# One step of a hybrid diffusion backbone: key latents inside the last block, adaLN rows turned later, a convolution's tanh in a slot of its own

## The chip, the cores and the metric

The kernel runs on one core of one Trainium2 chip. The metric is the time of the device for one execution, in microseconds (us). The core has a matrix engine (TensorE, PE in the profile), a vector engine (VectorE, DVE), a scalar engine (ScalarE, ACT), a third elementwise engine (GpSimd, POOL) and a queue engine that here issues the transfers (SyncE, SP). Each runs its own list of instructions in order; semaphores join them. PE writes its results into banks of PSUM, and a bank can be written again only when another engine has read it.

## What is computed

Two layers over 1024 latent tokens (with a grid position) and 256 context tokens, 1280 in all, width 1024. Each layer is RMSNorm, an adaLN shift and scale, a mixer, and a gated residual. The first mixer has windowed attention (A) and a matrix memory (mLSTM, B) side by side, the second is latent attention (C). What the change touches:

```
def _adaln(cond, w, b):
    m = jax.nn.silu(cond) @ w + b
    shift, scale, gate = jnp.split(m[:, None, :], 3, axis=-1)
...
    qk = jax.nn.silu(_dwconv_centred(jnp.concatenate([q, k], axis=-1), conv_w))   # mixer B
...
    q = (_rmsnorm(qa, q_norm) @ w_qb).reshape(B, T, C_HEADS, C_NOPE + C_ROPE)     # mixer C
    c_kv = _rmsnorm(kva, kv_norm)
    keys_ckv = jnp.concatenate([c_kv, cc], axis=1)
    keys_kr = jnp.concatenate([_axial_rope(kr, rows, cols), ckr[:, :, None, :]], axis=1)
    kv = (keys_ckv @ w_kvb).reshape(B, Tk, C_HEADS, C_NOPE + C_VDIM)
```

In C the keys are 1536: 1280 of the step (latents of width 256) and 256 from a cache.

## The kernel before

**Numbers.** Every float32 operand of a product is split into a high part in a shorter float type (fp32r) and the low rest, and a product is three matmuls: high x high, high x low, low x high. So each operand that is made costs a cast on ACT (names with h) and a subtraction on DVE or POOL (names with l): L576/L577 for weights, L1648/L1649 for v of mixer B, L820/L821 for the rotary parts of C, L2070/L2071 and L2067/L2068 for latents, keys, queries and values of C.

**Order.** The program is written as one stream. In three stretches (the start, the memory of B with dense blocks beside it, the windowed attention) the stream is the order, written by hand (`manual_schedule`). In the rest, to which the first layer's dense blocks behind the start and the entry of mixer C belong, the build itself sets in what order each engine gets the instructions, and only the dependencies are given.

**Dense blocks.** Products with the input weights go in blocks of 256 to 384 columns. A unit is one PSUM bank: 24 matmuls, eight depths of 128 by three. Tokens come in three chunks, 512, 512 and 256 (`CHUNKS`), or in ten tiles of 128 (tt). Beside the blocks run steps of the adaLN sums (`mod_sums`, L501 to L551): 64 small matmuls make four rows of sums in a bank, `columns` (L512) scales them on ACT (mrow, L514), turns them on PE (the transpose of L123) and adds the bias on DVE (B or A, L521). In the same stretch `gates` makes the memory's gates: scans over 1280 tokens on DVE (L1528 to L1535), then exponentials on ACT (gB, rst, gM; L1563, L1567, L1570), then turns of LI, rst and gM on PE, ten of them into each bank, copied out at L1591.

**Convolution of B** (`b_proj`, L1595). For each head the q and k blocks are followed by a convolution over three tokens. It goes in slots: `K.later(f, n)` puts f into the slot n further on; a slot holds the work of some unit and of the memory beside it. `taken` copies a bank into a ring tile (scr, L1609); a slot or more later `conv` (L1622) takes one of four cx tiles and writes the middle tap on ACT (L1626); a slot later `taps` adds the two others on DVE (L1629, L1630) and at once issues the tanh on ACT (L1632); a slot later `silu` multiplies on DVE (L1636); a slot later a transfer writes cx out (in<-cx, L154 on SP). Behind q and k come the units of v, which `v_split` casts on ACT (L1648) and subtracts on DVE (L1649).

**Entry of C** (`layer_c`). The last two dense blocks make the query latents (b = 0) and the key latents (b = 1), tile by tile (`latent`, L1987). A dict `K.behind` gives functions to run behind a tile (b, tt): `q_latent` turns the query latents of a chunk, `q_rope` (L2032) makes the rotary query part for four heads and one chunk (nine matmuls, then the rotation L770 to L773 and the split L820/L821), and `k_rope` the same for the keys' rotary part (32 rows). After the last unit the rest follows: `kv_latent` (L2020) turns the key latents of chunk 0, 1, 2 and of the cache (3) into the ckv tiles, four `q_rope`s for chunk 2, one `k_rope`, the weights' splits (L2278 to L2297), then `C.keys`, `C.queries` and `C.values`. The normalised tokens of the layer (hh0, hl0 and so on, chunk by chunk) are last read by the dense blocks.

Of the kernel before, what the change touches and what calls it, by code (L numbers as in the profile page):

```python
# [12 lines left out]
F32R = mybir.dt.float32r  # L13
# [13 lines left out]
KD = D // 128  # L27
# [473 lines left out]
def mod_sums(K, p, blocks):  # L501


    nc, cond = K.nc, cond_cols(K, p)
    at = lambda t, c: t[c::32]
    if any(f < 2 * D for _, f in blocks):
        bcol = K.t(p, [128, 16], F32, "bcol1", 1)
        K.dma(bcol, K.I["k_cols"][:, 96:112])
        nc.vector.tensor_scalar(bcol[:, 8:16], bcol[:, 8:16], 1.0, None, ALU.add)
        K.A[1], K.Bm[1] = [K.const.tile([128, 2, 8], F32, tag=f"{n}1", name=f"{n}1") for n in "AB"]  # L510

    def columns(ps, f):  # L512
        rows = K.t(p, [128, 128], F32, "mrow1", 2)
        nc.scalar.mul(rows, ps[:, 0:128], 0.5)  # L514
# [6 lines left out]
        nc.vector.tensor_add(dst, src, bc(bcol, 8 * a))  # L521
        if a:
            nc.vector.tensor_mul(dst, dst, bc(K.gcol, 8))

    def gate(ps, l, f, bias):
        nc.vector.scalar_tensor_tensor(bias, ps[:, 0:128], 0.5, bias, ALU.mult, ALU.add)
        for c in range(2):
            K.dma(K.modd[l][c, f:f + 512].rearrange("(q p) -> q p", p=128), at(bias, c))

    for l, f in blocks:  # L530
        ws, bias = [], None
        for i in range(8):
            for k in (2 * i, 2 * i + 1) if i < 4 else ():
                w = K.t(p, [128, 512], F32, "mw", 8)
                K.dma(w, K.I["w_mod"][l, k * 128:(k + 1) * 128, f:f + 512])
                ws.append(w)
            if i == 4 and f >= 2 * D:
                bias = K.t(p, [128, 128], F32, "bmod", 2)
                nc.gpsimd.memset(bias, 0.0)
                for c in range(2):  # L540
                    K.dma(at(bias, c), K.I["b_mod"][l, f:f + 512].rearrange("(q p) -> q p", p=128))
            if i == 7:
                ps = K.ps()
                for k in range(KD):
                    for q in range(4):
                        K.mm(ps[q * 32:q * 32 + 32, 0:128], cond[:, k, :], ws[k][:, q * 128:(q + 1) * 128], k == 0, k == KD - 1)
                if bias is None:
                    columns(ps, f)
                else:
                    gate(ps, l, f, bias)  # L550
            yield  # L551


class DenseBlock:
# [295 lines left out]
def layer_ab(K):  # L850
    nc, I = K.nc, K.I
    left, right = K.left, K.right
    d = K.d = {}
# [12 lines left out]
    hp = right("hT0")  # L866
# [93 lines left out]
        pass  # L960
    while opened:
        opened.pop().release()
    hp = K.hp1 = right("hT1")
    K.hTh, K.hTl = [], []
    for ci, (t0, N) in enumerate(CHUNKS):
        K.hTh.append(hp.tile([128, KD, N], F32R, tag=f"hh{ci}", name=f"h1Th{ci}"))
        K.hTl.append(hp.tile([128, KD, N], F32R, tag=f"hl{ci}", name=f"h1Tl{ci}"))
    wp = K.w1 = right("w1")
# [626 lines left out]
def b_proj(K, wp, h):  # L1595
# [26 lines left out]
    def conv(p, ci, qk, j):  # L1622
        t0, N = CHUNKS[ci]
        cw = K.cw[:, :, qk * 8 + 2 * h + j]
        x = K.t(K.cvp, [128, 512], F32, "cx", 4)[:, 0:N]
        nc.scalar.mul(x, p[:, 1:N + 1], cw[:, 1:2])  # L1626

        def taps():
            nc.vector.scalar_tensor_tensor(x, p[:, 0:N], cw[:, 0:1], x, ALU.mult, ALU.add)  # L1629
            nc.vector.scalar_tensor_tensor(x, p[:, 2:N + 2], cw[:, 2:3], x, ALU.mult, ALU.add)  # L1630
            th = K.sc(K.ring, [128, 512], F32, "cth")[:, 0:N]
            nc.scalar.activation(th, x, AF.Tanh, scale=1.0 if qk == 0 else 16.0)  # L1632
# [441 lines left out]
def layer_c(K):  # L2074
# [42 lines left out]
    for w, o in zip(pre, (0, 0, 256)):  # L2117
        K.dma(w, I["w_kvb_c"][0, :, o:o + 256].rearrange("(k p) (h a c) -> p k h a c", p=128, h=2, a=2))
    K.u = {}
    K.behind = {(0, 5): [partial(q_latent, K, 0)], (0, 9): [partial(q_latent, K, 1)], (1, 1): [partial(q_latent, K, 2)]}  # L2120
    for n in range(8):
        K.behind[1, n + 2] = [partial(q_rope, K, wr, n % 4, n // 4)]
    K.behind[1, 5].append(partial(k_rope, K, 0))
    K.behind[1, 9].append(partial(k_rope, K, 1))
    dense.run(2)
    K.w1.release()
    K.hp1.release()

    lp = right("lat")
    ckv = [[lp.tile([128, 2, 512], F32R, tag=f"ckv{s}{c}", name=f"ckv{s}{c}") for c in range(3)] for s in range(2)]  # L2130
    wp = right("cw")
    sets = [right("ckv0"), right("cvr")]
    C = Mla(K, wp, cq, ckv)
    C.weights(0, pre[0])
    C.weights_v(0, pre[1:])
    k_rope(K, 2)
# [93 lines left out]
class Mla:  # L2230
# [298 lines left out]
```

## Time and profile before

| what | value |
|---|---|
| median of 3 runs | 2583.2 us (2578.94, 2583.2, 2584.51) |
| the profiled execution | 2579.96 us, of which the span of the instructions is 2578.2 us |
| mean granted PE clock | 0.996 |
| HBM read and written | 233.49 MB and 110.50 MB |

PE is the busiest engine by far; how much of the span each engine is busy stands in the prediction's first lines. The page's busy rows by slices (40 slices of 64 us) show where the others come near it: DVE and ACT in the last third, which is the attention of C. A row of the waits' view reads: engine, operation and line that waited, then what it waited for, then us in total, times, and the longest. A row of a timeline reads: start, length, engine, line, operation, out<-in, how many, and in brackets the idle time before it and what ended that. A row of a stretch reads: from and to, length, busy us of each engine (and instructions), granted clock of PE (1.00 is full), share of the DMA engines, GB/s.

### The profile page before, as it was taken

What the parts mean: (1) busy time and instruction counts of PE and PEld (TensorE: products, weight loads), DVE (VectorE), ACT (ScalarE), POOL (GpSimd) and SP (SyncE); (2) the same over time, 40 slices, a digit from 0 to 9 for tenths busy, and PEclk for the clock granted to TensorE, in tenths of its full rate; (3) what the DMA queues carried; (4) which work ended last, traced back from release to release, by engine and by line L of the source; (5) the groups of instructions that cost most, each with busy time, mean ns of one, the idle gap of its engine ahead of it and who ended that gap; (6) DMA issues with size and microseconds to landing.
All of it is one profiled execution on the core that took longest, in us unless ns stands there. A gap on an engine that the chain in (4) does not pass through costs nothing.

```text
span 2578.2 us, 48626 instructions
## 1 busy us (share of the span) xinstructions
PE 2534.9 (98%) x16482; PEld 2248.8 (87%) x16482; DVE 1702.8 (66%) x3927; ACT 1442.0 (56%) x3664; POOL 1126.9 (44%) x1510
## 2 busy tenths in 40 slices
PE   8999999999999999999999999999999999999998
PEld 6998998998998888878888778898899999999887
DVE  6633655656657575677777456426888888888754
ACT  6423535535434432577666433233888888888842
POOL 6223233233225344366554543135455555555832
PEclk9999999999999999999999999999999999999999
DMA  7665576666577564465443455423210101101334
GB/s 267 209 196 162 155 215 180 182 202 178 160 220 225 182 215 150 113 171 161 127 124 97 162 160 165 126 70 120 66 39 28 43 28 43 33 30 28 122 100 133
DMA packets 338955, 347.21 MB, mean 135 GB/s; under 512 B 36409, under 2 KB 281838, under 8 KB 338450
## 3 DMA queue, kind: packets, MB, share of 16 engines
q1 hardware_dynamic: 338706, 344.10, 43.8%
q8 instruction: 131, 2.15, 0.3%
q14 instruction: 118, 0.97, 0.1%
HBM read 233.49 MB, written 110.50 MB: 133 GB/s over the span
## 4 chain that ended last, share of the span: by engine, by line
PE 89%; DVE 3%; DMA 2%; ACT 2%; issue 2%; POOL 1%; SPq 1%; POOLq 0%; DVEq 0%; ACTq 0%
PE mm L119 36%; PE S L119 31%; PE V L119 9%; PE T L123 7%; PE D L119 3%; PE mm L123 3%; PE T L119 1%; SPq L154 1%; POOL w L1068 0%; DMA w<-in_w_out_c 0%; DMA w<-in_w_out_ab 0%; DMA y<-w 0%; POOL wl L577 0%; DMA xin<-in_x_sample 0%; DVE gM L1535 0%
## 5 line engine op out<-in xcount | busy, mean ns | idle before, releaser
L577 POOL TENSOR_TENSOR wl<-wf,wh 128x256 fp32r<-128x256 f32 (+2 forms) x272 | 222.8, 845 | 496.7 <-ACT wh L576 432.9
L119 PE MATMUL mm<-hTh,wh 128*128 128x512 f32 (+1 forms) x912 | 329.2, 361 | 0.9 <-DVE scr L821 0.9
L119 PE MATMUL mm<-hTh,wl 128*128 128x512 f32 (+1 forms) x912 | 324.7, 356 | 0.0
L119 PE MATMUL mm<-hTl,wh 128*128 128x512 f32 (+1 forms) x912 | 324.1, 355 | 0.0
L119 PE MATMUL S<-cK,cQ 96*128 96x512 f32 (+3 forms) x1248 | 301.6, 365 | 0.8 <-ACT cPb L2421 0.4
L2469 DVE TENSOR_TENSOR cpl<-T,cph 128x512 fp32r<-128x512 f32 x336 | 227.8, 684 | 36.3 <-ACT cph L2468 32.5
L119 PEld LDWEIGHTS S<-cK,cQ 96*128 96x128 f32 (+1 forms) x1248 | 192.5, 189 | 20.7 <-ACT cPb L2421 1.7
L2468 ACT CAST cph<-T 128x512 fp32r<-128x512 f32 x336 | 192.4, 589 | 29.1 <-PE T L123 15.7
L119 PEld LDWEIGHTS mm<-hTh,wl 128*128 128x128 f32 x912 | 171.4, 188 | 27.0
L119 PEld LDWEIGHTS mm<-hTh,wh 128*128 128x128 f32 x912 | 171.5, 188 | 23.8 <-DVE scr L821 1.1
L119 PEld LDWEIGHTS mm<-hTl,wh 128*128 128x128 f32 x912 | 171.7, 188 | 23.2
L2419 DVE TENSOR_REDUCE cmx<-S 128x1 f32<-128x512 f32 x256 | 172.9, 682 | 20.6 <-PE S L119 18.9
L119 PE MATMUL V<-cph,cV 128*128 128x256 f32 x672 | 177.3, 289 | 1.0 <-ACT cph L2468 0.9
L119 PE MATMUL V<-cpl,cV 128*128 128x256 f32 x672 | 171.9, 284 | 0.8 <-DVE cst L2396 0.3
L1343 ACT CAST att_ph<-mm 128x512 fp32r<-128x512 f32 x168 | 98.6, 587 | 94.4 <-PE mm L123 92.6
L2400 POOL TENSOR_SCALAR cPa<-cPa,cst 128x512 f32<-128x512 f32 x128 | 98.3, 768 | 114.5 <-DVE cst L2397 94.3
L119 PE MATMUL mm<-wh,hTh 128*128 128x256 f32 x480 | 136.2, 284 | 3.3 <-DVE scr L1649 3.2
L1344 DVE TENSOR_TENSOR att_pl<-mm,att_ph 128x512 fp32r<-128x512 f32 x168 | 115.8, 689 | 35.7 <-ACT att_ph L1343 30.8
L119 PE MATMUL mm<-wl,hTh 128*128 128x256 f32 x480 | 135.7, 283 | 0.1
L119 PE MATMUL mm<-wh,hTl 128*128 128x256 f32 x480 | 135.2, 282 | 0.0
L119 PEld LDWEIGHTS V<-cph,cV 128*128 128x128 f32 x672 | 126.6, 188 | 7.9 <-ACT cph L2468 1.1
L119 PEld LDWEIGHTS V<-cpl,cV 128*128 128x128 f32 x672 | 126.7, 189 | 6.7 <-DVE cpl L2469 0.9
(459 smaller groups left out, 7737.1 us busy)
## 6 DMA issues: line engine op xcount, KB each, us to landing
wf<-in_w_in_ab SPq DMA_DIRECT2D x120, 256.0 KB
in<-in SPq DMA_DIRECT2D x40, 514.0 KB
in<-in SPq DMA_DIRECT2D x32, 386.0 KB
mw<-in_w_mod SPq DMA_DIRECT2D x48, 256.0 KB
in<-scr SPq DMA_DIRECT2D x40, 258.0 KB
o_x<-y SPq DMA_DIRECT2D x20, 512.0 KB
xin<-in_k_wmod SPq DMA_DIRECT2D x16, 512.0 KB
in<-cx SPq DMA_DIRECT2D x32, 256.0 KB
```

The source lines that it names most:

```text
L119: return self.nc.tensor.matmul(out, lhsT, rhs, start=start, stop=stop)
L123: self.nc.tensor.transpose(out, in_, self.ident[:p, :p])
L154: self.nc.sync.dma_start(f(out), f(in_))
L577: K.nc.gpsimd.tensor_sub(wl, wf[:, k], wh.bitcast(F32))
L1343: K.nc.scalar.copy(ph, self.T)
L1344: K.nc.vector.tensor_sub(pl, self.T, ph.bitcast(F32))
L2400: nc.gpsimd.tensor_scalar(pv, pv, wt[:, c:c + 1], rd, ALU.mult, ALU.mult)
L2419: nc.vector.tensor_reduce(mx[:, b, c:c + 1], S, AX.X, ALU.max, negate=True)
L2468: nc.scalar.copy(ph, T_)
L2469: nc.vector.tensor_sub(pl, T_, ph.bitcast(F32))
```

## The change

Three edits. (1) `columns` no longer turns its rows at once: it returns a function that does (`turned`), and the next block of adaLN sums calls it at its third step (i == 2); the last is called at the end. (2) In the convolution the tanh is put one slot behind the taps; the silu and the transfer behind it move a slot as well. (3) In layer C the first chunk of tokens gets a pool of its own (K.lat, tag hT1), and the tiles hh0 and hl0 are taken again for the key latents (`keys_latent`), so that `kv_latent` of chunk 0, 1 and the cache can run inside the last block, behind tiles (1, 5), (1, 9) and (1, 7). The eight `q_rope`s of chunks 0 and 1 get other places, two of them in the block before; the four of chunk 2 follow `kv_latent(2)` together. Two of the seven V tiles are the unused quarters of hh0 and hl0.

```
--- before.py
+++ after.py
@@ -512,6 +512,9 @@
     def columns(ps, f):
         rows = K.t(p, [128, 128], F32, "mrow1", 2)
         nc.scalar.mul(rows, ps[:, 0:128], 0.5)
+        return partial(turned, rows, f)
+
+    def turned(rows, f):
         pc = K.psT()
         K.tr(pc[:, 0:128], rows)
         a, k = f // D, f % D // 128
@@ -527,9 +530,12 @@
         for c in range(2):
             K.dma(K.modd[l][c, f:f + 512].rearrange("(q p) -> q p", p=128), at(bias, c))
 
+    late = None
     for l, f in blocks:
         ws, bias = [], None
         for i in range(8):
+            if i == 2 and late:
+                late = late()
             for k in (2 * i, 2 * i + 1) if i < 4 else ():
                 w = K.t(p, [128, 512], F32, "mw", 8)
                 K.dma(w, K.I["w_mod"][l, k * 128:(k + 1) * 128, f:f + 512])
@@ -545,10 +551,12 @@
                     for q in range(4):
                         K.mm(ps[q * 32:q * 32 + 32, 0:128], cond[:, k, :], ws[k][:, q * 128:(q + 1) * 128], k == 0, k == KD - 1)
                 if bias is None:
-                    columns(ps, f)
+                    late = columns(ps, f)
                 else:
                     gate(ps, l, f, bias)
             yield
+    if late:
+        late()
 
 
 class DenseBlock:
@@ -960,9 +968,11 @@
         pass
     while opened:
         opened.pop().release()
-    hp = K.hp1 = right("hT1")
+    K.lat = right("hT1")
+    hp = K.hp1 = right("hT2")
     K.hTh, K.hTl = [], []
     for ci, (t0, N) in enumerate(CHUNKS):
+        hp = K.hp1 if ci else K.lat
         K.hTh.append(hp.tile([128, KD, N], F32R, tag=f"hh{ci}", name=f"h1Th{ci}"))
         K.hTl.append(hp.tile([128, KD, N], F32R, tag=f"hl{ci}", name=f"h1Tl{ci}"))
     wp = K.w1 = right("w1")
@@ -1628,6 +1638,9 @@
         def taps():
             nc.vector.scalar_tensor_tensor(x, p[:, 0:N], cw[:, 0:1], x, ALU.mult, ALU.add)
             nc.vector.scalar_tensor_tensor(x, p[:, 2:N + 2], cw[:, 2:3], x, ALU.mult, ALU.add)
+            K.later(tanh)
+
+        def tanh():
             th = K.sc(K.ring, [128, 512], F32, "cth")[:, 0:N]
             nc.scalar.activation(th, x, AF.Tanh, scale=1.0 if qk == 0 else 16.0)
             K.later(lambda: silu(th))
@@ -2117,32 +2130,43 @@
     for w, o in zip(pre, (0, 0, 256)):
         K.dma(w, I["w_kvb_c"][0, :, o:o + 256].rearrange("(k p) (h a c) -> p k h a c", p=128, h=2, a=2))
     K.u = {}
+    ckv = [[], []]
+
+    def keys_latent(ci):
+        if not ci:
+            for t, nm in zip(ckv, ("hh0", "hl0")):
+                whole = K.t(K.lat, [128, KD, 512], F32R, nm)
+                t += [whole[:, k:k + 2, :] for k in range(0, KD, 2)]
+        kv_latent(K, ci, ckv)
+
     K.behind = {(0, 5): [partial(q_latent, K, 0)], (0, 9): [partial(q_latent, K, 1)], (1, 1): [partial(q_latent, K, 2)]}
-    for n in range(8):
-        K.behind[1, n + 2] = [partial(q_rope, K, wr, n % 4, n // 4)]
-    K.behind[1, 5].append(partial(k_rope, K, 0))
-    K.behind[1, 9].append(partial(k_rope, K, 1))
+    for n, at in enumerate(((0, 7), (0, 8), (1, 0), (1, 2), (1, 3), (1, 4), (1, 6), (1, 8))):
+        K.behind.setdefault(at, []).append(partial(q_rope, K, wr, n % 4, n // 4))
+    for f, ci, at in ((k_rope, 0, (1, 5)), (k_rope, 1, (1, 9))):
+        K.behind.setdefault(at, []).append(partial(f, K, ci))
+    for ci, tt in ((0, 5), (3, 7), (1, 9)):
+        K.behind.setdefault((1, tt), []).append(partial(keys_latent, ci))
     dense.run(2)
     K.w1.release()
     K.hp1.release()
 
-    lp = right("lat")
-    ckv = [[lp.tile([128, 2, 512], F32R, tag=f"ckv{s}{c}", name=f"ckv{s}{c}") for c in range(3)] for s in range(2)]
+    lp = K.lat
+    spare = [t.pop().rearrange("p k (i g a d) -> p (k i) g a d", i=2, g=2, a=2) for t in ckv]
     wp = right("cw")
     sets = [right("ckv0"), right("cvr")]
     C = Mla(K, wp, cq, ckv)
     C.weights(0, pre[0])
     C.weights_v(0, pre[1:])
     k_rope(K, 2)
-    for ci in range(4):
-        kv_latent(K, ci, ckv)
-        q_rope(K, wr, ci, 2)
+    kv_latent(K, 2, ckv)
+    for q in range(4):
+        q_rope(K, wr, q, 2)
     C.add_set(sets[0])
     p.release()
     cu.release()
     ap = C.ap = left("catt")
     C.add_queries(ap)
-    C.add_values(ap, sets[1])
+    C.add_values(ap, sets[1], spare=spare)
     for c in range(3):
         C.keys(0, c)
     C.queries(0, 0)
@@ -2249,11 +2273,11 @@
                 K.dma(keys[1][s][o:o + 32, :], kr[s])
         self.KV.append(keys)
 
-    def add_values(self, *pools):
+    def add_values(self, *pools, spare):
 
         n = 0
-        tiles = []
-        for pool, k in zip(pools, (3, 4)):
+        tiles = [*spare]
+        for pool, k in zip(pools, (3, 2)):
             tiles += [pool.tile([128, 4, 2, 2, 64], F32R, tag=f"cV{i}", name=f"cV{i}") for i in range(n, n + k)]
             n += k
         self.V = {(p, c): tiles[i] for p, row in enumerate(self.SLOTS) for c, i in enumerate(row)}
```

In the built program, on DVE, at the first adaLN row in the stretch with the gates: before, the bias add B stands right behind a tap of the convolution and ahead of v's constants (scr<-unit).

```order
L1630 SCALAR_TENSOR_TENSOR cx_1865<-scr_1861,cw,cx_1865 128x256
L521 TENSOR_TENSOR B_1144<-T_2017,bcol_242_1140 128x4x2
L1568 TENSOR_TENSOR dl<-dl,mp 36x10
L1650 CAST scr_1977<-unit 128x2x2
L1650 CAST scr_2032<-unit 128x2x2
```

On DVE at the same place, now:

```order
L1649 SCALAR_TENSOR_TENSOR cx_1865<-scr_1869,cx_1865 128x256
L1662 TENSOR_TENSOR scr_1977<-S_1913,scr_1977 128x256
L1662 TENSOR_TENSOR scr_2029<-S_1926,scr_2029 128x256
L1662 TENSOR_TENSOR scr_2046<-S_1939,scr_2046 128x256
L1662 TENSOR_TENSOR scr_2067<-S_1952,scr_2067 128x256
L1663 CAST scr_2142<-unit 128x2x2
L524 TENSOR_TENSOR B_1144<-T_2106,bcol_242_1140 128x4x2
L1662 TENSOR_TENSOR scr_2101<-S_2076,scr_2101 128x256
```

The add has moved behind the silu and four low parts of v (scr, from the banks S). On PE, the turn of the row itself (T<-ident,mrow; S are the banks of v's units) before:

```order
L119 MATMUL S_1939<-wh_1487,hTh_127 128x256
L123 MATMUL T_2017<-ident,mrow_366_2015 128x128
L119 MATMUL S_1939<-wl_1488,hTh_127 128x256
L119 MATMUL S_1939<-wh_1487,hTl_128 128x256
L119 MATMUL S_1952<-wh_1475,hTh_127 128x256
```

And on PE now, with the turn 38 rows later, behind the whole next unit of v:

```order
L119 MATMUL S_2076<-wl_1488,hTh_129 128x256
L119 MATMUL S_2076<-wh_1487,hTl_130 128x256
L123 MATMUL T_2106<-ident,mrow_366_2015 128x128
L119 MATMUL S_2113<-wh_1455,hTh_129 128x256
L119 MATMUL S_2113<-wl_1456,hTh_129 128x256
```

Here the two last matmuls of one unit, all twelve of the next one's second half and the 24 of a further unit have come ahead of the turn.

On ACT in the memory stage, at the last head's change from k to v, before (ho and kwh belong to the memory, mm are the banks of v):

```order
L1860 ACTIVATE ho_9317<-S_9211,hr_9313 128x256
L1626 ACTIVATE cx_9319<-scr_9153,cw 128x256
L1632 ACTIVATE scr_9323<-cx_9236 128x512
L1648 CAST scr_9327<-mm_9173 128x256
L1648 CAST scr_9331<-mm_9186 128x256
L1648 CAST scr_9335<-mm_9268 128x256
```

On ACT, now:

```order
L1873 ACTIVATE ho_9313<-S_9207,hr_9309 128x256
L1636 ACTIVATE cx_9315<-scr_9149,cw 128x256
L1645 ACTIVATE scr_9321<-cx_9147 128x512
L1661 CAST scr_9323<-mm_9169 128x256
L1661 CAST scr_9327<-mm_9182 128x256
L1661 CAST scr_9331<-mm_9264 128x256
L1803 CAST sd_9387<-um_8990 128x2x128
L1811 CAST Ch_9390<-Cs_8106 128x516
L1645 ACTIVATE scr_9396<-cx_9232 128x512
```

The tanh ahead of the three casts belongs to another buffer: cx_9147, whose taps are in the slot before. That of the newest 512 tokens (cx_9232, scr_9396) has moved behind the casts.

On PE at the entry of C, now, from the keys' products (S from hh and hl, which hold the latents) to the first queries (mm from cq):

```order
L119 MATMUL S_22696<-hh_4699_22306,wkl_22566 128x512
L119 MATMUL S_22696<-hh_4699_22306,wkh_22565 128x512
L123 MATMUL T_22584<-ident,u_22446 128x128
L119 MATMUL S_22696<-hl_4700_22307,wkh_22565 128x512
L119 MATMUL S_22696<-hh_4699_22306,wkl_22566 128x512
L123 MATMUL T_22589<-ident,u_22446 128x128
L123 MATMUL T_22584<-ident,u_22505 128x128
L123 MATMUL T_22589<-ident,u_22505 128x128
L119 MATMUL mm_23026<-cq_20447,wqh_22561 128x512
```

Before, the queries stood behind nine further rows of turns and products; the last q_ropes now stand ahead of this piece. On POOL at the same place, now (wkl, wvl and wql are the low parts of weights, rp_s and rp_t the rotation, ur a power):

```order
L2306 TENSOR_TENSOR wkl_22566<-wk_21517,wkh_22565 128x256
L2321 TENSOR_TENSOR wvl_22570<-wk_21518,wvh_22569 128x2x128
L2321 TENSOR_TENSOR wvl_22570<-wk_21519,wvh_22569 128x2x128
L780 TENSOR_TENSOR rp_s_22524<-rp_s_22524,rtabc 32x512
L2011 TENSOR_TENSOR ur_22510<-ur_22510,mhalf 128x1
L829 TENSOR_TENSOR rp_t_22469<-rp_t_22469,so_h_22475 128x512
L2303 TENSOR_TENSOR wql_22562<-wq_22559,wqh_22561 128x384
L781 TENSOR_TENSOR rp_t_22523<-rp_t_22523,rp_s_22524 32x512
L2017 TENSOR_TENSOR cko_22515<-u_22505,kvb 128x256
```

The rotation of the second k_rope's part (rp_s and rp_t of 32 rows) stands with the weights' low parts in one queue, its sum (rp_t<-rp_t,rp_s) behind wql; before, one more rotation 128 wide stood between them.

More of the change, by code (lines that the diff above doesn't have):

```diff
@@ L514, in columns, with turned @@
         nc.scalar.mul(rows, ps[:, 0:128], 0.5)
+        return partial(turned, rows, f)
+    def turned(rows, f):
         pc = K.psT()
@@ L528, in gate @@
             K.dma(K.modd[l][c, f:f + 512].rearrange("(q p) -> q p", p=128), at(bias, c))
+    late = None
     for l, f in blocks:
@@ L532, in mod_sums @@
         for i in range(8):
+            if i == 2 and late:
+                late = late()
             for k in (2 * i, 2 * i + 1) if i < 4 else ():
@@ L547, in mod_sums @@
                 if bias is None:
-                    columns(ps, f)
+                    late = columns(ps, f)
                 else:
@@ L551, in mod_sums @@
             yield
+    if late:
+        late()
 class DenseBlock:
@@ L962, in layer_ab @@
         opened.pop().release()
-    hp = K.hp1 = right("hT1")
+    K.lat = right("hT1")
+    hp = K.hp1 = right("hT2")
     K.hTh, K.hTl = [], []
     for ci, (t0, N) in enumerate(CHUNKS):
+        hp = K.hp1 if ci else K.lat
         K.hTh.append(hp.tile([128, KD, N], F32R, tag=f"hh{ci}", name=f"h1Th{ci}"))
@@ L1630, in taps, with tanh @@
             nc.vector.scalar_tensor_tensor(x, p[:, 2:N + 2], cw[:, 2:3], x, ALU.mult, ALU.add)
+            K.later(tanh)
+        def tanh():
             th = K.sc(K.ring, [128, 512], F32, "cth")[:, 0:N]
@@ L2119, in layer_c, with keys_latent @@
     K.u = {}
-    K.behind = {(0, 5): [partial(q_latent, K, 0)], (0, 9): [partial(q_latent, K, 1)], (1, 1): [partial(q_latent, K, 2)]}
[L2121 to L2124, printed above, removed]
+    ckv = [[], []]
+    def keys_latent(ci):
+        if not ci:
+            for t, nm in zip(ckv, ("hh0", "hl0")):
+                whole = K.t(K.lat, [128, KD, 512], F32R, nm)
+                t += [whole[:, k:k + 2, :] for k in range(0, KD, 2)]
+        kv_latent(K, ci, ckv)
+    K.behind = {(0, 5): [partial(q_latent, K, 0)], (0, 9): [partial(q_latent, K, 1)], (1, 1): [partial(q_latent, K, 2)]}
+    for n, at in enumerate(((0, 7), (0, 8), (1, 0), (1, 2), (1, 3), (1, 4), (1, 6), (1, 8))):
+        K.behind.setdefault(at, []).append(partial(q_rope, K, wr, n % 4, n // 4))
+    for f, ci, at in ((k_rope, 0, (1, 5)), (k_rope, 1, (1, 9))):
+        K.behind.setdefault(at, []).append(partial(f, K, ci))
+    for ci, tt in ((0, 5), (3, 7), (1, 9)):
+        K.behind.setdefault((1, tt), []).append(partial(keys_latent, ci))
     dense.run(2)
@@ L2127, in layer_c @@
     K.hp1.release()
-    lp = right("lat")
-    ckv = [[lp.tile([128, 2, 512], F32R, tag=f"ckv{s}{c}", name=f"ckv{s}{c}") for c in range(3)] for s in range(2)]
+    lp = K.lat
+    spare = [t.pop().rearrange("p k (i g a d) -> p (k i) g a d", i=2, g=2, a=2) for t in ckv]
     wp = right("cw")
@@ L2136, in layer_c @@
     k_rope(K, 2)
-    for ci in range(4):
-        kv_latent(K, ci, ckv)
-        q_rope(K, wr, ci, 2)
+    kv_latent(K, 2, ckv)
+    for q in range(4):
+        q_rope(K, wr, q, 2)
     C.add_set(sets[0])
@@ L2144, in layer_c @@
     C.add_queries(ap)
-    C.add_values(ap, sets[1])
+    C.add_values(ap, sets[1], spare=spare)
     for c in range(3):
@@ L2250, in add_set, with add_values @@
         self.KV.append(keys)
-    def add_values(self, *pools):
+    def add_values(self, *pools, spare):
         n = 0
-        tiles = []
-        for pool, k in zip(pools, (3, 4)):
+        tiles = [*spare]
+        for pool, k in zip(pools, (3, 2)):
             tiles += [pool.tile([128, 4, 2, 2, 64], F32R, tag=f"cV{i}", name=f"cV{i}") for i in range(n, n + k)]
```

## The prediction

> **What bounds the kernel now.** I read the page's busy times first, then the view of what TensorE (PE) waited for, then the busy time and granted clock in chosen stretches of 3.41 us, and only then the timelines around each wait.
>
> ```profile
> span 2578.2 us, 48626 instructions
> PE 2534.9 (98%) x16482; PEld 2248.8 (87%) x16482; DVE 1702.8 (66%) x3927; ACT 1442.0 (56%) x3664; POOL 1126.9 (44%) x1510
> PE T L123 <- ACT mrow L514: 5.0, 2, 4.6
> PE mm L119 <- DVE scr L1649: 3.2, 1, 3.2
> PE T L123 <- DVE ckv L2071: 1.8, 4, 0.6
> ```
>
> PE is busy for 2534.9 of 2578.2 us. No matmul is removed by the change, so it can win only from the 43.3 us of idle and from time that PE ran on a halved clock. The change aims at three places: the adaLN rows (5.0 us in 2 waits, the longer 4.6), one eviction in the convolution stage (3.2 us), and the entry of the last layer (ckv and its neighbours). The second cost is in the stretches (columns: length, then busy us of PE, PEld, DVE, ACT, POOL, then granted clock, DMA share, GB/s):
>
> ```profile
> 138.44:141.86 3.42, 0.00 (x1) 0.00 (x0) 3.29 (x7) 1.51 (x4) 0.36 (x1) 1.00 0.81 176
> 145.27:148.69 3.42, 3.42 (x18) 3.42 (x18) 2.94 (x10) 2.63 (x3) 0.00 (x0) 0.50 0.84 185
> 148.69:152.10 3.41, 3.41 (x30) 3.41 (x30) 2.33 (x8) 1.75 (x7) 0.00 (x0) 1.00 0.96 318
> 677.75:681.16 3.41, 0.44 (x3) 0.44 (x4) 3.02 (x8) 2.66 (x8) 0.20 (x1) 1.00 0.22 71
> 681.16:684.58 3.42, 3.42 (x18) 3.42 (x17) 2.81 (x7) 0.84 (x2) 0.00 (x0) 0.50 0.62 216
> 1148.80:1155.60 6.80, 5.40 (x34) 3.99 (x33) 5.26 (x14) 5.45 (x14) 3.34 (x5) 1.00 0.74 216
> 1790.50:1793.91 3.41, 1.51 (x9) 0.79 (x8) 2.57 (x6) 2.79 (x7) 2.68 (x3) 1.00 0.35 126
> 1793.91:1800.74 6.83, 6.19 (x16) 4.63 (x16) 3.11 (x9) 2.65 (x8) 3.40 (x7) 0.50 0.63 177
> 1786.00:1800.74 14.74, 11.28 (x44) 7.82 (x43) 8.81 (x19) 7.76 (x17) 9.94 (x12) 0.77 0.50 153
> 1700.00:1786.00 86.00, 86.00 (x558) 82.45 (x557) 39.94 (x87) 31.71 (x85) 37.74 (x44) 1.00 0.21 66
> ```
>
> A stretch with 3.42, 2.97 (3.41 - 0.44) or 1.90 (3.41 - 1.51) us of PE idle is followed by one at clock 0.50; the two from 1148.80 with 1.40 together (6.80 - 5.40) are at 1.00 and stay there. So a stall costs itself and, from somewhere between 1.4 and 1.9 us in one stretch, a half-clock stretch too. Its price: PE gets through 18 matmuls instead of 30 in 3.4 us, a loss of 0.4 x 3.41 = **1.4 us** for each such stretch of work.
>
> **The adaLN rows (first edit).**
>
> ```profile
> 143.04 0.48 PE L123 MATMUL T<-ident,mrow 128*128 128x128 f32 x1 [4.59 <-ACT mrow L514]
> 153.80 0.79 PE L123 MATMUL T<-ident,rst 36*128 36x36 f32 x10
> 142.73 0.25 ACT L514 ACTIVATE mrow<-S 128x128 f32<-128x128 f32 x1
> 147.33 1.27 ACT L1567 ACTIVATE rst<-rst 36x1280 f32<-36x1280 f32 x1
> 147.62 0.16 DVE L521 TENSOR_TENSOR B<-T,bcol 128x8 f32<-128x8 f32 x1
> 149.28 1.41 DVE L1649 TENSOR_TENSOR scr<-S,scr 128x256 fp32r<-128x256 f32 x4
> 1782.30 3.79 PE L119 MATMUL S<-cq,wr 128*128 128x256 f32 x30
> ```
>
> PE stops at 138.45 (143.04 - 4.59) because ACT makes the row only at 142.73. A 256-wide matmul at full clock takes 0.12 us (the row with 30 of them, 3.79 / 30, less the drain of the last). The order puts 38 such matmuls ahead of the turn: 138.45 + 38 x 0.12 = 143.0, when the row is ready (142.98). That wait goes. But something else is late next. After the turn come 24 matmuls (2.9, to 145.9) and the ten turns of LI (as many as those of rst, which take 0.79 with the drain: 0.7, to 146.6). The turns of rst need the exponential of L1567 (147.33 + 1.27 = 148.60) and the PSUM bank that the adaLN turn has used. Its reader, L521 (B), ran at 147.62; in the new order it stands on DVE behind the four low parts of v, which end at 149.28 + 1.41 = 150.69, so the bank is free at about 150.9. These DVE and ACT times hang on the gate scans, not on PE, and I keep them. PE reaches the rst turns at 151.0 instead of 153.80, a gain of 2.8, with a **new stall of 4.4 us** (146.6 to 151.0). It puts over 2 us of idle into each of two stretches, so I charge the rest of 148.69:152.10 (1.1 x 0.4) and one whole stretch: 1.8. Net -1.0; the shorter wait of the same kind (5.0 - 4.6) goes as well, -0.4. **Sum -1.4**; ends -3.2 (no half clock) and 0 (one half stretch more). The turns that move in other blocks had waited for nothing; their cover is the matmuls around them.
>
> **The convolution (second edit).**
>
> ```profile
> ACT scr L1632 <- DVE cx L1630: 45.5, 39, 4.3
> 665.55 0.38 SPq L154 DMA_DIRECT2D in<-cx  x1
> 670.32 0.72 ACT L1626 ACTIVATE cx<-scr,cw 128x512 f32<-128x512 f32 x1 [0.32 <-DMA in<-cx]
> 671.27 0.44 SPq L154 DMA_DIRECT2D in<-cx  x1
> 674.41 0.64 ACT L1632 ACTIVATE scr<-cx 128x512 f32<-128x512 f32 x1 [3.36 <-DVE cx L1630]
> 679.32 0.63 ACT L1632 ACTIVATE scr<-cx 128x512 f32<-128x512 f32 x1 [0.75 <-DVE cx L1630]
> 679.86 0.90 ACT L1648 CAST scr<-mm 128x256 fp32r<-128x256 f32 x3
> 680.24 0.42 DVE L1649 TENSOR_TENSOR scr<-mm,scr 128x256 fp32r<-128x256 f32 x1 [0.36 <-ACT scr L1648]
> ```
>
> The 3.2 us wait ends with L1649 at 680.24, after the casts of L1648, which stood on ACT behind a tanh that waited 0.75 us for DVE. With the tanh one slot later that wait goes. What is added: the four cx buffers stay in use a slot longer, while the next L1626 of a buffer keeps its slot. The order now has the transfer of a buffer just one slot ahead of the L1626 that overwrites it. Such a transfer took 670.32 - 665.55 = 4.77 us from issue to release. If the one issued at 671.27 takes as long, L1626 starts at 676.04 in place of the tanh at 674.41. Behind it on ACT stand the copies and scalings of the state update, on which DVE and the next hr wait, then the casts. L1626 (0.72) and a 256-wide tanh (about 0.4) then end at 677.1, where today's tanh ends at 674.95: everything behind is 2.1 later, and with today's 0.75 gone and a scaling already done the casts come 1.2 later, at 681.1. If the transfer lands by 674.4, they come some 0.5 earlier, but then DVE's taps and one silu bind and leave 0.3. Ends -0.3 and +1.2; I take **+0.3**, nearer to the early end: 4.77 belongs to the one transfer here that stopped ACT, so the others landed before they were missed. The half stretch behind the stall stays (2.97 of idle would have to lose a whole microsecond).
>
> **The last layer's entry (third edit).**
>
> ```profile
> 1780.94 1.15 PE L123 MATMUL T<-ident,u 128*32 128x128 f32 x9
> 1780.27 0.75 POOL L2282 TENSOR_TENSOR wkl<-wk,wkh 128x256 fp32r<-128x256 f32 x1
> 1780.97 1.89 POOL L2297 TENSOR_TENSOR wvl<-wk,wvh 128x256 fp32r<-128x256 f32 x2
> 1782.82 0.54 POOL L1998 TENSOR_TENSOR ur<-ur,mhalf 128x1 f32<-128x1 f32 x1
> 1783.34 1.28 POOL L821 TENSOR_TENSOR rp_t<-rp_t,so_h 128x512 fp32r<-128x512 f32 x1
> 1784.59 1.07 POOL L2279 TENSOR_TENSOR wql<-wq,wqh 128x384 fp32r<-128x384 f32 x1
> 1788.24 1.56 POOL L772 TENSOR_TENSOR rp_s<-rp_s,rtabc 32x512 f32<-32x512 f32 x1 [0.64 <-DVE rp_s L771]
> 1791.00 1.25 POOL L773 TENSOR_TENSOR rp_t<-rp_t,rp_s 32x512 f32<-32x512 f32 x1
> 1792.29 0.62 ACT L820 CAST so_h<-rp_t 32x512 fp32r<-32x512 f32 x1 [0.59 <-POOL rp_t L773]
> 1793.26 0.41 DVE L821 TENSOR_TENSOR rp_t<-T,so_h 32x256 fp32r<-32x256 f32 x1 [0.73 <-ACT so_h L820]
> ```
>
> Here today's loss is 14.74 - 11.28 = 3.46 us of idle and 0.4 x 6.19 = 2.5 us of half clock: 6.0. The latents and two q_ropes move into the last block's units, where PE has no idle at all (86.00 of 86.00), DVE, ACT and POOL are under half busy, and the two V tiles that take over latent buffers add no instruction. If that cover were short, PE would wait there for a low part (L821) of at most 1.28 us. Let X be the end of the last unit. PE then has 12 turns (0.1 each, as in the row of nine: 1.2), 36 matmuls 256 wide (4.4), 2 turns, 6 products of the keys 512 wide (twice 0.12, 1.4) and 4 turns: 7.6 us of work. Next come the queries of `C.queries`, in the PSUM bank of the last k_rope's turn. That bank is freed by DVE's L821 behind ACT's so_h, which stands on ACT behind the so_h of the k_rope before it, and this waits for POOL's queue: from about X + 0.9 (the cast of wkh) the rows above, 0.75 + 1.89 + 1.56 + 0.54 + 1.28 + 1.07 + 1.25 = 8.34, so X + 9.2; two so_h (0.62 and, at half the width, about 0.35) and the low part (0.41) make X + 10.6. A **new stall of 3.0 us** takes the place of the seven small ones, and I charge one half stretch: 4.4 in place of 6.0. **Sum -1.6**; ends -6.0 (POOL's queue is done in time) and +1.0 (a second half stretch, or ACT held by a so_h). The attention behind it is planned anew in small swaps of rows: 0, between -1 and +1.
>
> **The sum.** -1.4 + 0.3 - 1.6 = -2.7 us. The profiled execution took 2579.96 (1.8 around its span), so 2577.3 for such a run; the runs shown have a median of 2583.2 and lie from 2578.94 to 2584.51, and the mean of all four is 2581.7. From that mean: **2579.0**.
>
> **A rule beside it.** The stretch at 1790.50 has idle in pieces (the waits for ckv are 0.6 at most), 1.90 in all, and the clock still halves behind it. The Trainium skill (TensorE: Matmul & The Clock Gate, "Why this matters for your kernels") asks only that no gap between bursts exceed some 3 us, one idle window bringing the half rate. This trace is stricter than that. By the page the entry's stall of 3.0 would be just short of a halving and the sum 1.4 lower.
>
> **Rivals.** (1) *Clean stretches*: the clock halves only behind a gap near 3 us, so that the entry goes free, or POOL's queue at the entry is shorter than I add up. For it: two of the three new stalls rest on queue sums. Against: the stretch at 1790.50. It gives -3.2 - 0.3 - 1.6 - 1.4 = -6.5 to -9.5: 2572 to 2575; chance 0.38. (2) *Slower*: the buffers of cx. In the other heads too, ACT stands in L1626 for a transfer while copies and casts wait behind it, and PE finds the banks full. Price: at four of the six changes from q to k and from k to v in three heads 1.2 + 1.4 for a half stretch, 10.4; with the gains of 3.0 +7.4: 2589. It decides where the banks cover less than 1.2 us. Against it: tanh waited 45.5 us for taps on ACT in 39 places and only one reached PE. Chance 0.09. (3) *Nothing moves*: each stall reappears at full price (the rst turns, the casts, the bank at the entry): 2581 to 2583, chance 0.08. My forecast has 0.45.
>
> **Numbers.** The range takes in the ends: -10.5 (3.2 + 0.3 + 6.0 + 1) from the lowest run gives 2568, +3.2 from the median 2586. A measurement of this kernel can tell about 0.2%, here 5.2 us, from no change. Faster by more: all of (1) and a little of the forecast, 0.41; within: 0.51; slower: most of (2), 0.08.
>
> **What would show it.** In the changed profile: the wait of the turns for mrow gone, a wait of the rst turns for B of some 4 us with clock 0.50 behind it; an L1626 on ACT idle for in<-cx near 675 and the casts within 1.2 us of 679.86; PE idle about 3 us ahead of the first queries, behind POOL's L773 and two so_h. The forecast is wrong if the rst turns wait under 1.5 us, if the entry has no single wait over 1.5 us, or if waits for L1649 appear in other heads.

## The result, and the profile after

The changed kernel is slower. Its median is 2604.72 us (five runs, 2602.42 to 2605.99) against 2583.2 us for the kernel before (five runs, 2578.94 to 2586.23): a ratio of 1.0086, with a 95% interval from 1.0071 to 1.0101. That is 21.5 us more, where the prediction had 2579.0 and a range up to 2586. The profiled execution took 2602.42 us.

The page of the changed kernel answers the two rows that opened the prediction:

```profile
span 2600.6 us, 48623 instructions
...
PE 2535.3 (97%) x16482; PEld 2247.5 (86%) x16482; DVE 1701.5 (65%) x3927; ACT 1439.4 (55%) x3664; POOL 1129.1 (43%) x1510
```

PE does the same 16482 matmuls in the same busy time (2535.3 against 2534.9 us). The span has grown by 22.4 us, and PE's idle time by 22.0 (65.3 against 43.3). So the loss is idle time, and the view of what PE waited for says where (engine, operation and line, what it waited for, us in total, times, the longest):

```profile
PE mm L119 <- ACT o_ah L1066: 12.9, 1, 12.9
PE T L123 <- DVE xin L335: 8.6, 2, 7.9
PE mm L119 <- DVE w L1077: 5.8, 7, 0.9
PE T L123 <- DVE B L524: 4.0, 1, 4.0
PE mm L119 <- DVE scr L1662: 3.5, 1, 3.5
PE V L119 <- DVE co L2508: 2.8, 3, 1.5
PE mm L119 <- DVE rp_t L829: 2.4, 1, 2.4
```

The waits for B, scr and rp_t are the three that the prediction speaks of. The second row, at the start of the program, was there before (8.8 us). New, and in no step of the prediction, are the first, third and sixth: 12.9 + 5.8 + 2.8 = 21.5 us. They lie together, from the end of the attention of mixer C into the output products behind it. Stretches of the changed kernel there (from and to, length, busy us of PE, PEld, DVE, ACT, POOL, then granted clock, DMA share, GB/s):

```profile
2395.00:2455.00 60.00, 58.81 (x429) 53.47 (x427) 51.66 (x123) 50.85 (x142) 37.33 (x65) 1.00 0.07 23
2455.00:2459.75 4.75, 2.25 (x17) 1.84 (x16) 2.29 (x5) 1.58 (x4) 0.73 (x1) 1.00 0.08 28
2459.75:2476.82 17.07, 3.83 (x10) 2.43 (x9) 3.07 (x3) 6.55 (x11) 9.78 (x8) 0.50 0.82 270
2476.82:2535.00 58.18, 52.36 (x221) 40.56 (x220) 18.30 (x33) 12.61 (x27) 18.41 (x16) 1.00 0.37 122
```

The same part of the program in the kernel before:

```profile
2395.00:2455.00 60.00, 58.26 (x361) 50.19 (x360) 43.77 (x101) 47.03 (x125) 45.17 (x62) 1.00 0.41 128
2455.00:2476.82 21.82, 21.82 (x127) 18.91 (x126) 12.68 (x26) 10.06 (x26) 9.38 (x12) 1.00 0.26 87
2476.82:2512.60 35.78, 35.78 (x200) 30.91 (x199) 20.40 (x42) 15.74 (x42) 14.96 (x19) 1.00 0.30 100
```

Read the DMA columns first. Before, transfers ran beside the attention (share 0.41, 128 GB/s from 2395 to 2455), and from 2455 on PE had no gap. Now the transfers are all but absent until 2455 (0.07, 23 GB/s), and then they fill the engines (0.82, 270 GB/s) while PE stands still. From 2455.00 to 2535.00 PE idles 2.50 + 13.24 + 5.82 = 21.6 us, and the 3.83 us that it works between 2459.75 and 2476.82 are at half clock (0.50), which is about another 1.9.

**Which transfers.** SP's own timeline shows them. The loads of the output weights come in pairs (`wq`, `wk`, later `w`). Before:

```profile
2389.70 0.33 SPq L154 DMA_DIRECT2D wq<-in_w_out_c  x1
2393.15 0.33 SPq L154 DMA_DIRECT2D wk<-in_w_out_c  x1
...
2401.90 1.37 SPq L154 DMA_DIRECT2D w<-in_w_out_c  x3
```

And after:

```profile
2386.52 0.33 SPq L154 DMA_DIRECT2D wq<-in_w_out_c  x1
2389.99 0.33 SPq L154 DMA_DIRECT2D wk<-in_w_out_c  x1
...
2458.82 1.35 SPq L154 DMA_DIRECT2D w<-in_w_out_c  x3
2460.21 0.43 SPq L154 DMA_DIRECT2D fn<-in_final_norm  x1
```

Up to the `wq` the changed kernel is 3.2 us ahead (2386.52 against 2389.70), near the 2.7 of the prediction's sum, though a lead read from two single executions has its own scatter. The loads of `w` that follow are 56.9 us late (2458.82 against 2401.90).

**Why they are late.** These loads are made by a function that the prediction never looked at, `weights_out`, which runs in the slots of the last pair of heads (pair 7):

```
            if i == 6:
                while late:
                    late.pop(0)()
                for pool in (sets[1], sets[0], wp, lp):
                    pool.release()
                p = fin["p"] = right("fin")
...
    SLOTS = ((3, 4, 5), (0, 1, 2), (3, 5, 0), (4, 6, 1), (0, 2, 4), (3, 5, 1), (4, 6, 3), (0, 2, 1))
```

At its seventh step it gives back four pools (`lp` is the latents' pool) and lays a new one, `fin`, with the tiles of `w` in their place. `SLOTS` has a row for each pair of heads: the numbers of the V tiles that hold the pair's values for the three chunks of keys. A tile in the new pool can be written only when the last reader of what lay there has finished. The last pair reads its values from V tiles 0, 1 and 2. Before, these three lay in the query pool (`catt`, `ap`), which stays, and only tiles 3 to 6 in a pool that is given back. The change counts the two spare tiles first (`tiles = [*spare]`), so numbers 0 and 1 are now the quarters of hh0 and hl0, in `K.lat`, the very pool that is released. So the loads of `w` can come only at the end of the attention's products with these tiles. In the built order the first of them stands on SP right behind the attention's transfer caT<-csz of 2458.40 and is issued 0.9 us before the last product with `hl` (2459.75); on which of the old tiles each load lies, the traces don't show. PE at that point, after:

```profile
2459.75 0.41 PE L119 MATMUL V<-cpl,hl 128*128 128x256 f32 x1
2473.04 1.22 PE L119 MATMUL mm<-cq,o_ah 128*128 128x512 f32 x2 [12.88 <-ACT o_ah L1066]
2474.62 0.79 PE L119 MATMUL mm<-cq,o_al 128*128 128x512 f32 x1 [0.35 <-DVE o_al L1067]
```

The names say it: the last value product reads `hl`, a former token tile; behind it comes the first output product, after 12.88 us of idle. SP and ACT show what lies in between, after:

```profile
2463.07 0.84 SPq L154 DMA_DIRECT2D o_a<-caT  x1
2461.79 1.30 ACT L2207 CAST w<-w 128x512 fp32r<-128x512 f32 x2 [1.21 <-DMA w<-in_w_out_c]
2465.20 0.62 ACT L2207 CAST w<-w 128x512 fp32r<-128x512 f32 x1 [2.12 <-DMA w<-in_w_out_c]
2470.82 1.32 ACT L2207 CAST w<-w 128x512 fp32r<-128x512 f32 x2 [5.00 <-DMA w<-in_w_out_c]
2472.37 0.62 ACT L1066 CAST o_ah<-o_a 128x512 fp32r<-128x512 f32 x1 [0.23 <-DMA o_a<-caT]
```

The first output product does not need `w` itself (its weights are the three depths in `cq` that were loaded earlier). It needs o_ah, the cast of o_a. That cast stands on ACT behind casts of `w` that wait for their transfers, but the last thing that it waits for itself, another 0.23 us, is its own operand: o_a is a tile of the new pool too, and its load is issued at 2463.07, behind the first loads of `w` in SP's list, and lands only at about 2472.35, 9.28 us later, while the transfers fill the engines. So the wait that the page names (ACT o_ah) is one for transfers, of o_a last and of `w` just before it. In the kernel before, the load of o_a and the same product came here:

```profile
2407.60 0.47 SPq L154 DMA_DIRECT2D o_a<-caT  x1
2417.05 0.73 PE L119 MATMUL mm<-cq,o_ah 128*128 128x512 f32 x2
```

From the first load of `w` to the first product it was 15.15 us then (2417.05 - 2401.90) and 14.22 now (2473.04 - 2458.82). The way has not become longer. It has lost its cover: the four output tiles that were written into the slots of the last pair, and the loads ahead of them, now stand behind the attention with nothing beside them.

### The profile page after: what moved, and what is told of

Read it like the earlier page. It is cut to its first block, busy times and chain, and to the rows that moved or that the text cites. A ratio compares the mean times of both kernels' runs of the same rounds, so it can differ in the third digit from the quotient of the medians.

```text
span 2600.6 us, 48623 instructions
## 1 busy us (share of the span) xinstructions
PE 2535.3 (97%) x16482; PEld 2247.5 (86%) x16482; DVE 1701.5 (65%) x3927; ACT 1439.4 (55%) x3664; POOL 1129.1 (43%) x1510
## 4 chain that ended last, share of the span: by engine, by line
PE 84%; DVE 3%; DMA 2%; issue 2%; ACT 2%; POOL 1%; SPq 1%; DVEq 0%; POOLq 0%; ACTq 0%
PE mm L119 35%; PE S L119 28%; PE V L119 9%; PE T L123 7%; PE D L119 3%; PE mm L123 3%; SPq L154 1%; PE T L119 1%; DMA o_a<-caT 0%; DMA y<-w 0%; DVE w L1077 0%; DMA w<-in_w_out_ab 0%; DVE cmx L2443 0%; POOL w L1078 0%; DMA att_q<-ql 0%
## 5 line engine op out<-in xcount | busy, mean ns | idle before, releaser
L1342 POOL TENSOR_SCALAR att_p<-att_p,att_den 128x640 f32<-128x640 f32 (+1 forms) x128 | 97.8, 778 | 81.1 <-DVE att_den L1339 28.2
L584 ACT CAST wh<-wf 128x256 fp32r<-128x256 f32 (+2 forms) x272 | 96.3, 409 | 59.5 <-DMA wf<-in_w_in_c 28.9
L119 PE MATMUL V<-cph,cV 128*128 128x256 f32 x464 | 123.2, 289 | 0.0
L119 PE MATMUL V<-cpl,cV 128*128 128x256 f32 x464 | 119.5, 284 | 0.3 <-DVE cst L2417 0.3
```

Of the source, the lines that this page charges most:

```text
L119: return self.nc.tensor.matmul(out, lhsT, rhs, start=start, stop=stop)
L584: K.nc.scalar.copy(wh, wf[:, k])
L1342: nc.gpsimd.tensor_scalar(pv, pv, den[:, i:i + 1], 1.0, ALU.mult, ALU.mult)
```

## The experiments

**The theory.** The loss of some 25 us is the place of two V tiles: counted first, they are read last, in a pool that is wanted for the output weights. **The rival.** The moved latents themselves cost it: more work in the last block, another plan of the attention, and the late loads only a result of that. A third possibility was that the loss had several sources among the three edits. The diffs are from the changed kernel, but for experiment 4. Each ratio is to runs of the kernel before that were made beside the experiment: 21 for experiments 1 to 4 (median 2580.58 us), 35 for experiments 5 to 8 (median 2581.36), which ran on another chip. Experiment 1 was not run again there, so it is compared with 5 to 8 by the ratios alone.

**1. The spare tiles counted last** (all three edits kept). The last pair then has its values in 0, 1 and 2 as before, in the pool that stays.

```
-        tiles = [*spare]
+        tiles = []
         for pool, k in zip(pools, (3, 2)):
...
+        tiles += spare
```

> All three edits stay; only the list of V tiles is turned round: the two spare tiles (in the pool of the key latents) come last in place of first, so that the last pair of heads keeps its values in tiles of the query pool, as in the kernel before. Theory (the last pair's values lie in the pool that the output weights must take over, so their loads wait for the last matmul on V): the loads of w go back to about 2400 us, no wait of 12.9 us, no half clock from 2459.75; the time falls by about 24 us to 2578 to 2581, a little below the kernel before. Rival A (the new place of the latents or the moved work has made the tail late by itself): 2595 to 2605, loads still near 2458.

Measured: 2577.43 us (2575.89 to 2582.25), a ratio to the kernel before of 0.9986 (0.9977 to 0.9995). The late loads and the long wait are gone; its SP timeline has

```profile
2398.37 1.37 SPq L154 DMA_DIRECT2D w<-in_w_out_c  x3
```

and the longest waits of its PE, behind the start's xin, are the three of the forecast; all that follow are 2.3 us or less:

```profile
PE T L123 <- DVE B L524: 4.0, 1, 4.0
PE mm L119 <- DVE scr L1662: 3.0, 1, 3.0
PE mm L119 <- DVE rp_t L829: 2.4, 1, 2.4
```

Two lines undo the loss, with every edit still in the kernel. The rival, that the latents' move in itself makes the loss, falls with it.

**2. Without the third edit** (the latents behind the last unit as before; the turns and the tanh as changed).

```
-    K.lat = right("hT1")
-    hp = K.hp1 = right("hT2")
+    hp = K.hp1 = right("hT1")
...
-    kv_latent(K, 2, ckv)
-    for q in range(4):
-        q_rope(K, wr, q, 2)
+    for ci in range(4):
+        kv_latent(K, ci, ckv)
+        q_rope(K, wr, ci, 2)
...
-        tiles = [*spare]
-        for pool, k in zip(pools, (3, 2)):
+        tiles = []
+        for pool, k in zip(pools, (3, 4)):
```

> The kernel before with the first two edits alone (adaLN rows later, tanh later); the entry of C as before. Theory: these two are worth -0.4 us together by the trace (the new stall of the rst turns eats the old one), so 2582 to 2584, the same as before. Rival B (the first two edits have part in the loss): 2588 or more.

Measured: 2580.12 us (2577.53 to 2586.55), ratio 1.0001 (0.9992 to 1.001). No loss, and no gain that can be told from none.

**3. The third edit alone** (the turns and the tanh as before).

```
-    late = None
...
-            if i == 2 and late:
-                late = late()
...
-            K.later(tanh)
-
-        def tanh():
```

> The third edit alone. Theory: it holds the whole loss, 2603 to 2607, and a wait of PE for o_ah of 11 to 14 us. Rival B: some 2595 to 2600.

Measured: 2606.39 us (2604.5 to 2608.08), ratio 1.0099 (1.0085 to 1.0112). The loss is whole, and the wait for o_ah is there with 13.2 us. Of the three edits it is the third that brings it.

**4. The kernel before, with nothing but the place of its V tiles changed.** The pool that is given back holds tiles 0 to 3, the one that stays 4 to 6. None of the three edits is in it.

```
-    C.add_values(ap, sets[1])
+    C.add_values(sets[1], ap)
...
-        for pool, k in zip(pools, (3, 4)):
+        for pool, k in zip(pools, (4, 3)):
```

> The kernel before, none of the edits, but its seven V tiles taken in the other order: four from the pool that is released for the output weights first, then three from the query pool, so that the last pair's values lie in the released pool. Theory: the loss appears without any of the edits, +20 to +28 us: 2603 to 2611, with the loads of w near 2460. Rival A: 2583, as before.

Measured: 2606.67 us (2603.27 to 2608.69), ratio 1.0099 (1.0085 to 1.0113). What its PE waited for, in the rows that the kernel before doesn't have:

```profile
PE mm L119 <- ACT o_ah L1056: 12.8, 1, 12.8
...
PE mm L119 <- DVE w L1067: 5.8, 7, 0.9
...
PE V L119 <- DVE co L2484: 2.8, 3, 1.5
```

These are the three rows of the changed kernel to a tenth of a microsecond (12.9, 5.8, 2.8), and the load starts as late:

```profile
2461.97 1.34 SPq L154 DMA_DIRECT2D w<-in_w_out_c  x3
```

So the place of the tiles makes the loss alone, without the latents, the turns or the tanh. Experiment 1 takes it out of the changed kernel and this one puts it into the old one.

The other four runs stand on experiment 1 and ask about the three local terms.

**5. The adaLN turn two steps later still** (i == 4). The forecast said that the turn's bank is late because its reader stands behind v's low parts; with the turn behind the gates' turns that bank should no longer matter.

```
-            if i == 2 and late:
+            if i == 4 and late:
```

> On top of e1_spare_last: the adaLN row is turned at the fifth step of the next block in place of the third, so that in the built order the turn stands behind the turns of LI, rst and gM. Theory (the rst turns wait for B, because the adaLN turn has their bank): the wait of 4.0 us for B goes, the rst turns wait for their exponential only, near 148.6 + launch offset, some 2.0 us, and the half clock behind is one stretch at most: 2 to 4 us less than e1_spare_last, 2573 to 2576. Rival C (the rst turns are late for another reason, such as the low parts of v): no gain, the wait stays near 4.

Measured: 2576.12 us (2571.01 to 2578.72), ratio 0.9976 (0.9967 to 0.9985), against 0.9986 without it. The wait for B (4.0) is gone, and what stands in its place is the exponential that the forecast had as the second limit:

```profile
PE T L123 <- ACT rst L1577: 1.8, 1, 1.8
```

By the ratios that is 2.6 us better than experiment 1, in line with the 2.2 us of wait that go; the intervals of the two overlap.

**6. The tanh back in the taps' slot** (the second edit undone).

```
-            K.later(tanh)
-
-        def tanh():
```

> On top of e1_spare_last: the second edit undone, the tanh again at once behind the taps. Theory (the tanh's own slot trades a wait for DVE against a wait for the transfer of cx): time within 1 us of e1_spare_last; ACT's waits for the transfer in<-cx fall from 24.3 us to about 3, its waits of the tanh for DVE come back to about 45, and PE's wait for the casts stays at 3 to 3.5 us. Rival D (the second edit is what gains): 2 to 4 us slower than e1_spare_last.

Measured: 2579.24 us (2575.11 to 2581.65), ratio 0.9994 (0.9985 to 1.0003), 0.0008 over experiment 1: some 2 us, with intervals that overlap, so whether the edit gains anything isn't settled. What it does on ACT is clear. With the tanh back, ACT waits so:

```profile
ACT scr L1642 <- DVE cx L1640: 47.3, 42, 4.5
ACT cx L1636 <- DMA in<-cx: 3.6, 2, 2.9
```

With the tanh in its own slot (experiment 1):

```profile
ACT cx L1636 <- DMA in<-cx: 24.3, 10, 4.8
ACT scr L1645 <- DVE cx L1640: 13.4, 8, 3.9
```

The edit trades 34 us of waiting for taps (47.3 - 13.4) for 21 us of waiting for the transfer that frees a cx tile (24.3 - 3.6). PE's wait at this place is 3.2 us without the edit and 3.0 with it.

**7. The second k_rope two tiles earlier**, to shorten the chain in front of the first queries.

```
-    for f, ci, at in ((k_rope, 0, (1, 5)), (k_rope, 1, (1, 9))):
+    for f, ci, at in ((k_rope, 0, (1, 5)), (k_rope, 1, (1, 7))):
```

> On top of e1_spare_last: the second k_rope stands behind tile (1, 7) in place of (1, 9), so that its rotation is ahead of the weights' low parts in POOL's queue. Theory (the first queries wait for the bank behind POOL's queue): the wait of 2.4 us for rp_t goes or falls under 1 us and with it the half stretch: 2 to 4 us less than e1_spare_last. Rival E (something else frees the bank late, such as ACT's casts of latents): the wait stays above 1.5 us.

Measured: 2577.19 us (2572.6 to 2581.0), ratio 0.9987 (0.9978 to 0.9996). The wait of 2.4 us for rp_t is gone from the rows, but the time is that of experiment 1 (0.9986): a miss. Its profiled execution happened to be the fastest of its eleven (span 2570.8); had that one been compared with experiment 1's profile (2574.5), it would have shown a gain that the medians don't have. Why the removed wait brings nothing in the median was not found.

**8. Both of these** (5 and 7 on experiment 1).

```
-            if i == 2 and late:
+            if i == 4 and late:
...
-    for f, ci, at in ((k_rope, 0, (1, 5)), (k_rope, 1, (1, 9))):
+    for f, ci, at in ((k_rope, 0, (1, 5)), (k_rope, 1, (1, 7))):
```

> f1_turn_later_still and f3_krope_earlier together on e1_spare_last. Theory: the two add up, 4 to 8 us less than e1_spare_last, 2570 to 2574, and 0.3 to 0.5% under the kernel before.

Measured: 2575.18 us (2569.43 to 2578.83), ratio 0.9974 (0.9964 to 0.9983). It has the lowest ratio here, 0.26% under the kernel before and, by the ratios, 1.1% under the changed one. By the ratios it is 3.1 us better than experiment 1, where 4 to 8 were hoped for, and its interval overlaps with those of experiments 1 and 5. One wait in it is new, in the attention:

```profile
PE V L119 <- ACT cph L2493: 2.9, 1, 2.9
```

It stands in experiment 2 as well, with 3.1 us, and is at most 0.9 in the others; what decides it stays open.

## Why the prediction was wrong, point by point

**The step that failed** is in the part on the last layer's entry: "the two V tiles that take over latent buffers add no instruction", and, at the end of that part, "The attention behind it is planned anew in small swaps of rows: 0, between -1 and +1." The first is true and was the wrong question. A tile costs no instruction, but where it lies decides what has to wait until it has been read for the last time. The term was set at 0 and is about +25: the changed kernel lies 3.2 us ahead at the load of `wq` and ends 22.4 us behind. From that load to the end PE is busy for 184.43 of 214.08 us, where it was busy for 179.81 of 188.50. So of these 25.6 us 21.0 are more idle time, nearly all of it between 2455 and 2535, and 4.6 are longer busy time; about 1.9 of that is the half clock, and the other 2.7 stay open. Experiments 1 and 4 show the cause, from both sides.

What would have found it ahead of the run: the diff shows the new count of the tiles, the table of `SLOTS` names the last readers, and the release in `weights_out` names the pools. The order of the loads on SP at the end of mixer C and what each waits for needed reading as much as PE at the entry. A first idea of the price was in the old trace: 15.15 us from load to first product, all of it under the cover of attention.

**The three local terms** came out near their sum. Forecast -2.7 us; with the tiles put right (experiment 1) the ratio of 0.9986 is -3.6 us, between -5.9 and -1.3. None of the three is settled by a run of its own, so the agreement of the sum may be partly luck.

*The adaLN rows.* The wait for mrow is down from 4.6 to 0.4 us, and the new stall stands where it was put, behind B:

```profile
151.92 0.94 PE L123 MATMUL T<-ident,rst 36*128 36x36 f32 x10 [4.02 <-DVE B L524]
```

Forecast were 4.4 us of stall and an end at 151.0. Over 2 us of idle in each of two stretches was forecast too; the changed kernel has 1.0 in the one up to 148.93 and 3.0 (3.41 - 0.42) in the next, and one stretch at half clock follows:

```profile
148.93:152.34 3.41, 0.42 (x7) 0.45 (x8) 2.61 (x12) 2.60 (x9) 0.00 (x0) 1.00 0.93 258
152.34:155.75 3.41, 3.41 (x20) 3.34 (x19) 1.09 (x3) 0.00 (x0) 0.00 (x0) 0.50 1.03 377
```

By the waits this is 4.0 + 0.4 in place of 5.0, and there is one half-clock stretch in place of two (5.65 us of work from 141.86 to 148.69 before, 3.41 now). At the prediction's price of 0.4 for each us of half clock that makes 0.6 + 0.9 = 1.5 us, close to the forecast 1.4. It is an estimate from two profiles and no measured gain.

*The convolution.* ACT stops for the transfer as described, and the casts follow, in the changed kernel:

```profile
674.41 0.72 ACT L1636 ACTIVATE cx<-scr,cw 128x512 f32<-128x512 f32 x1 [5.32 <-DMA in<-cx]
...
679.40 0.91 ACT L1661 CAST scr<-mm 128x256 fp32r<-128x256 f32 x3
```

The forecast had 674.4 for a transfer that is in time and 676.04 for one as slow as the one measured, and took a value between. By the clock time it was the early end, and the casts come 0.46 earlier than before (679.40 against 679.86). But the whole program is 0.6 us ahead here (the activation of ho just before starts at 665.17 in place of 665.76), so against what goes before the casts are 0.1 later. The transfer took 4.05 us from issue to release (670.36 to 674.41), a little less than the 4.77 of the slow one. PE's stall is 3.5 us in place of 3.2, which is the +0.3 of the forecast, and the half clock behind it stays, as said. The same stall is 3.0 in experiment 1 and 3.2 in experiment 6, so a few tenths say little. The rival that priced this edit at +10 elsewhere fell: PE waits for the casts of v in this one place only.

*The entry.* The seven small waits are one, for the low part of the rotation, as the prediction said it would be, of 2.43 us where 3.0 were forecast; the half stretch that was charged for it follows in experiment 1 and not in the changed kernel (last section). Between experiments 2 and 1 the third edit gains 0.15%, 3.9 us, with an interval of 0.09% to either side of each ratio; the forecast was 1.6, with ends of -6.0 and +1.0. So the mechanism was right, and the gain lies at the larger side if it is anything.

Alone, edits (1) and (2) were forecast at -1.1 us; experiment 2 has +0.3 with an interval of 2 us to either side, which leaves that undecided. Of the chances, 0.08 stood for slower, priced at 2589; it rested on the one mechanism (the cx tiles) that did no harm, and a loss of this size was in no rival.

## What to carry to other kernels

When a change moves data into another buffer, follow the buffer and not only the instructions: who reads it last, when its space is wanted again and by which load, and how long the chain from that load to the first use is when nothing covers it. A term of nothing for an edit of placement needs the same working as any other, above all at the end of a program, where loads for the last stage are laid over what the stage before still reads. And a wait that the profile puts down to a cast can be one for the transfers in front of that cast: of its own operand, and of what stands further up that engine's list.

## What the runs showed of the hardware

The halved clock doesn't follow from the length of a stall alone. The entry's stall of 2.43 us is the same in the changed kernel and in experiment 1. In the changed kernel it is cut by the end of a stretch, with 1.78 us (3.41 - 1.63) in the one and the rest before, and the next is at full clock:

```profile
1787.33:1790.74 3.41, 2.76 (x18) 2.17 (x17) 1.57 (x2) 0.94 (x3) 3.41 (x4) 1.00 0.21 77
1790.74:1794.15 3.41, 1.63 (x7) 1.38 (x8) 2.25 (x5) 2.30 (x7) 1.88 (x2) 1.00 0.56 173
1794.15:1797.57 3.42, 3.42 (x17) 2.79 (x16) 0.85 (x2) 0.73 (x3) 0.00 (x0) 1.00 0.41 129
```

In experiment 1 it falls whole into one stretch, with 2.43 us of idle (3.41 - 0.98), and the next is halved:

```profile
1788.00:1791.41 3.41, 0.98 (x5) 0.86 (x5) 2.57 (x5) 2.37 (x6) 2.53 (x3) 1.00 0.50 154
1791.41:1794.83 3.42, 3.42 (x9) 2.63 (x8) 0.50 (x2) 0.69 (x2) 0.00 (x0) 0.50 0.48 148
```

The Trainium skill (TensorE: Matmul & The Clock Gate, "Why this matters for your kernels") asks that gaps stay under some 3 us; by that neither stall would have cost a halving, so these rows are stricter, as the prediction's reading of the old trace was. Nor is the idle time of one stretch, laid out in this way, quite enough to tell: the 1.78 us above passed, and experiment 5 has 1.76 (3.42 - 1.66) in one stretch, and there a halving follows and lasts for two. In these rows the change lies near 1.8 us, and they don't place it more closely:

```profile
148.27:151.69 3.42, 1.66 (x20) 1.41 (x19) 2.72 (x9) 2.78 (x4) 0.00 (x0) 1.00 0.90 192
151.69:158.52 6.83, 6.83 (x41) 6.52 (x41) 3.44 (x11) 1.76 (x8) 0.00 (x0) 0.50 1.01 340
```

The stretches are 3.41 us long, laid out from the edges where the granted clock changes. With some 1.4 us a halved stretch, as the prediction worked it out, to be won or lost at each stall by where it falls, a few such places would be enough for the scatter of several microseconds between runs of one kernel. That is an argument; no run here tests it.
